# A two-layer mixer trunk on one core: pooling steps dealt out among tiles, two plain tiles ahead of the first seven-product pair, value-row transposes in another bank

## The chip, the cores and the metric

The kernel runs on one core of one Trainium2 chip. The metric is the device time of one execution in microseconds. TensorE (PE, with its weight loads PEld), VectorE (DVE), ScalarE (ACT), GpSimd (POOL) and the DMA queues each run their own instruction stream; streams meet at semaphores.

## The reference, cut to what matters

Two layers run over 640 tokens (128 context, 512 latent), model width 1024. Per layer:

```python
h = rmsnorm(x, norm1_g) * (1 + sc1) + sh1
attn, conv, pool, sgu = four mixers of h @ w_in          # widths 512 each
for i in range(4):                                       # gates and branches
    merged += sigmoid(h @ w_gate[i] + b_gate[i]) * (branch[i] @ w_branch[i])
x = x + g1 * (merged @ w_out)
h = rmsnorm(x, norm2_g) * (1 + sc2) + sh2
x = x + g2 * (square(relu(h @ w_mlp_in)) @ w_mlp_out)    # hidden width 4096
```

The pooling mixer takes 4 groups of 128 channels. For each it forms a centred window sum (windows 2, 4, 8, 16), divides by the number of tokens in the window, subtracts the token itself and multiplies by a 128x128 matrix. The convolution mixer is depthwise with 31 taps, then a layer norm over 512 channels. Attention needs the values by rows (tokens on partitions), while the kernel holds everything else with channels on partitions.

## The kernel before, in words

Channels lie on partitions, the 640 tokens on the free axis, in two halves of 320 columns. Every fp32 operand is split into a high and a low part (`split`, L237 to L241: ACT copies the high part `h`, DVE subtracts it to give the low part `l`), and every product takes three matmuls (h·h, h·l, l·h). A full tile (`mtile`) is 8 chunks x 3 x 2 halves = 48 matmuls of 128x320; a branch or output tile has 4 chunks, so 24. It accumulates in tag `ps` of PSUM, of which there are two; `sc`, `pt` and `po` have one each outside attention. A tile can start only when the tile two before it has been evicted from `ps`.

Weights come as slabs of 128x1024 in the order that `_order` writes down, through 4 `raw` buffers and 3 pairs of split buffers, and `advance` loads 3 slabs ahead and splits 2 ahead. The instruction orders of PE and of the SP DMA queue are those of the program text. DVE, ACT and POOL are ordered by a scheduler with priorities (`later(-n)` raises them), except that DVE too has the order of the text from the pooling stage to the middle of the last gates (`byhand`).

**Value rows.** After `qk`, five transposes in `v_rows` (L832) write a tile of tag `sc`, which two ACT copies (L838) and two DVE subtractions (L839) evict. The tile of tag `sc` used just before holds the sum of squares of q (L413) and is read by the reciprocal root's second step (L400). Next on PE is `conv_in(1)`, in half tiles of 24 matmuls, of tag `ps`.

**Pooling and convolution.** The stage is `gates(3)`, four tiles ("p", g), `branch(3)`, `gates(2)` (with `pool_out` in between), `branch(2)`, gates 1, `branch(1)`. The 31 x 4 convolution taps (L982, one DVE instruction each) are dealt out by `tick`: 5 after a gate, 2 after a branch tile, 6 after each of the first two tiles of gates 1, and the rest there. `pool_in` (L1072) evicts a tile with ACT, then writes DVE's additions (L1086, one to four), four small POOL products (L1092), two DVE instructions (L1096) and a split, all in one go, with no tap in between. `branch` evicts each tile with L1134 and adds it with L1136. `conv_out` sums the four convolution results (L992), takes a column sum on PE (L413), subtracts and squares, takes a second column sum, normalises; its three steps are taken after tiles 1, 2 and 4 of gates 1. In layer 0, `tick` also drives `mod_steps`, which puts small matmuls (L446), transposes and DMAs between the tiles.

**The MLP of layer 1 (`fast_mlp`).** Two tiles of hidden channels are made as a pair with seven products of quarter size (12 matmuls each, L651) in place of eight. That takes sums of quarters of the activations (`ta`, `tb`, L625 to L636, made once at the start on DVE and split) and of the weights (`Feed.pair`, L326 to L334, for each pair). Four plain tiles i0 to i3 come first, then 14 pairs, with output tiles (24 matmuls, evicted into `x` by L553) between the products. The first pair has a branch of its own in the text: two products, four output tiles, five products. `Feed` loads and splits all slabs from the first pair on.

```python
take = {(6, 1): 1, (7, 0): 1, (7, 1): 0}     # output slabs that a pair carries, else 2
```

Of the kernel before, what the change touches and what calls it, by code (L numbers as in the profile page):

```python
# [11 lines left out]
AF = mybir.ActivationFunctionType  # L12
# [3 lines left out]
P = 128  # L16
# [6 lines left out]
TH = T // 2  # L23
# [35 lines left out]
def _pairs():  # L59


    due = [(b, mp) for b in range(6) for mp in range(4)]
    take = {(6, 1): 1, (7, 0): 1, (7, 1): 0}
    r = []
    for b in range(1, 8):
        for p in range(2):
            n = take.get((b, p), 2)
            r.append((b, p, due[:n]))
            del due[:n]
    assert not due  # L70
    return r
# [5 lines left out]
def _order(l):  # L77

    r = [("k", 0), ("v", 0)] + [("q", i) for i in range(4)] + [("a", i) for i in range(8)]
    gate = lambda b: [("g", b, m) for m in range(8)]  # L80
    branch = lambda b: [("b", b, m) for m in range(4)]
    r += gate(0) + [("sv", i) for i in range(4)] + branch(0) + [("u", i) for i in range(4)]
    r += gate(3) + [("p", i) for i in range(4)] + branch(3)
    r += gate(2) + branch(2) + gate(1) + branch(1)
    r += 2 * [("o", m) for m in range(8)]
    if l in FAST:
        r += [("i", j) for j in range(4)]
        for b, p, fs in PAIRS:
            r += [("i", 4 * b + 2 * p + i) for i in range(2)] + [("h", *f) for f in fs]
        return r + 2 * [("f", 3, m) for m in range(8)]  # L90
    r += [("i", j) for j in range(8)]
    for b in range(4):
        if b < 3:
            r += [("i", 8 * (b + 1) + j) for j in range(8)]
        r += [("f", b, m) for m in range(8)] * (2 if b == 3 else 1)
    return r
# [17 lines left out]
def _run(g):  # L114

    try:
        while True:
            next(g)
    except StopIteration as e:
        return e.value  # L120
# [19 lines left out]
def trunk(ctx, tc, a, o):  # L140
# [436 lines left out]
    def first(keys, h, ss1, ab, keep=None):  # L577

        g = mtiles(keys, h, BY_CHUNK if ss1 is None else BY_HALF)
        while True:  # L580
            try:
                at = next(g)
            except StopIteration as e:
                return e.value
            if ss1 is not None and at == (0, 2):
                normed(h, 1, norm_stats(ss1), *ab, keep=keep)
            if nxt["cap"] == 2 and at == (1, 1):
                tick()
                tick()
            if nxt["cap"] == 2 and at == (1, 3):  # L590
                flush()
                pool.dma_start(out=lcol[1], in_=a["cols"][1])
                nxt["cap"] = len(order)

    def fast_mlp(l, mp, h, ss1, ab, fslot, relu2):

# [4 lines left out]
        keep = [ys[c % 4][:, TH * (c // 4):TH * (c // 4) + TH] for c in range(KC)]  # L601
        vs = first([("i", j) for j in range(3)], h, ss1, ab, keep)
        fd = Feed(mp)
        fd.base = fd.slab = nxt["use"] + 1
        todo, i = [], fd.base
        for b, p, fs in PAIRS:
            todo.append(fd.pair(i, [i + 2 + n for n in range(len(fs))]))
            i += 2 + len(fs)
        fd.tail = {n: fd.plain(n) for n in range(i, len(order))}
        fd.pump(2)  # L610
        f = [relu2(v) for v in vs]

        v = _run(mtile(use("i", 3), h))
        feed.append(fd)
        fd.pump()
        f.append(relu2(v))


        tslot = maker(mp, "t", 16, T)
# [37 lines left out]
                vec.tensor_tensor(out, v, s, ALU.add)  # L657
            return out

        fs_, due = {0: f}, []  # L660
        for (b, p, outs), q in zip(PAIRS, todo):
            nxt["use"] += 2 + len(outs)
            ks = dict(zip(outs, q["f"]))
            for n, (fb, mp_) in enumerate(outs):
                for m in (2 * mp_, 2 * mp_ + 1):
                    due.append((fb, m, nxt["use"] - len(outs) + n, ks[fb, mp_]))

            def out_tile():
                if not due:
                    return  # L670
                fb, m, n, k = due.pop(0)
                w = tuple(z.rearrange("p (k c) -> p k c", c=P) for z in ready[n])
                v = _run(mtile(w, fs_[fb], k0=4 * (m % 2)))
                for half in range(2):
                    residual(x[m], v[:, HALVES[half][0]:], mod3(l, 5), m, half)
                if m % 2:
                    ready.pop(n)
                    fd.finish(k)

            if (b, p) == PAIRS[0][:2]:  # L680
                p1, r1, c1, c2 = prod("pt", q["w1"], 0, b11), tmp(TH), tmp(T), tmp(T)
                with later(-EVAC_FIRST):
                    act.activation(r1, p1, AF.Copy)
                plus(prod("sc", q["w1"], 4, b21), r1, c1[:, a0:a1])
                fd.finish(q["k1"])
                for _ in range(4):
                    out_tile()
                p3 = prod("sc", q["w2"], 4, b22)
                p5 = prod("po", q["w4"], 0, t1)
                u2 = plus(prod("pt", q["w2"], 0, t2), r1)  # L690
                fd.finish(q["k2"])
                u3 = plus(prod("pt", q["w3"], 0, t3), u2)
                plus(p5, u2, u2)
                plus(p5, u3, c2[:, b0:b1])
                plus(p3, u2, c1[:, b0:b1])
                plus(prod("pt", q["w3"], 4, t4), u3, c2[:, a0:a1])
                fd.finish(q["k3"])
            else:
                p1, r1 = prod("pt", q["w1"], 0, b11), tmp(TH)
                with later(-EVAC_FIRST):  # L700
                    act.activation(r1, p1, AF.Copy)
                p5 = prod("po", q["w4"], 0, t1)
                out_tile()
                u2 = plus(prod("pt", q["w2"], 0, t2), r1)
                c1 = tmp(T)
                plus(prod("sc", q["w1"], 4, b21), r1, c1[:, a0:a1])
                fd.finish(q["k1"])
                out_tile()
                u3 = plus(prod("pt", q["w3"], 0, t3), u2)
                c2 = tmp(T)  # L710
                plus(p5, u2, u2)
                plus(p5, u3, c2[:, b0:b1])
                out_tile()
                plus(prod("pt", q["w3"], 4, t4), u3, c2[:, a0:a1])
                fd.finish(q["k3"])
                plus(prod("sc", q["w2"], 4, b22), u2, c1[:, b0:b1])
                fd.finish(q["k2"])
                out_tile()
            fb = fs_.setdefault(b, [])
            for c in (c2, c1):  # L720
                s = tmp(T)
                vec.scalar_tensor_tensor(s, c, 0.0, c, ALU.max, ALU.mult)
                fb.append(split(s, fslot, T))
            fb[-2:] = fb[:-3:-1]
# [16 lines left out]
    def qk(l, h, ap, pending, between):  # L741
# [88 lines left out]
        pool.dma_start(out=o["nv"][l], in_=vf[:, 0:SEQ])  # L830

        def v_rows():  # L832
            pt = psum("sc")
            for b in range(5):
                pe.transpose(pt[:, b * P:(b + 1) * P], vf[:, b * P:(b + 1) * P], ident)
            pv = pt[:, 0:T].rearrange("p (b v d) -> p b v d", b=5, v=2)
            for kv in range(NKV):
                act.activation(v5[:, 0:5, kv, 0, :], pv[:, :, kv, :], AF.Copy)  # L838
                vec.tensor_tensor(v5[:, 0:5, kv, 1, :], pv[:, :, kv, :], f5[:, 0:5, kv, 0, :], ALU.subtract)  # L839
# [229 lines left out]
        return split(y, bslot[0], T)  # L1069


    def pool_in(g, h, mk):  # L1072
        v = yield from mtile(use("p", g), h)
        b = tmp(PB)
        for p0, p1 in ((0, PP), (PP + SEQ, 2 * PP + SEQ), (PB - PP, PB)):
# [1 line left out]
        parts = ((0, SEQ, PP), (SEQ, T, 2 * PP + SEQ))  # L1077
        for c0, c1, b0 in parts:
            act.activation(b[:, b0:b0 + c1 - c0], v[:, c0:c1], AF.Copy)
        w = WINDOWS[g]  # L1080
        cur, n, st = b, PB, 1
        bufs = [tmp(PB), tmp(PB)]
        while st < w:
            n -= st
            nx = bufs[0]
            vec.tensor_tensor(nx[:, 0:n], cur[:, 0:n], cur[:, st:st + n], ALU.add)  # L1086
            cur, st = nx, 2 * st
            bufs.reverse()
        off = PP - w // 2
        fx = pfix[:, g * 32:(g + 1) * 32]  # L1090
        for f0, b0 in ((0, 0), (8, SEQ - 8), (16, SEQ + PP), (24, SEQ + PP + LAT - 8)):
# [2 lines left out]
        for c0, c1, b0 in parts:  # L1094
            o0 = b0 - PP + off
            vec.scalar_tensor_tensor(z[:, c0:c1], cur[:, o0:o0 + c1 - c0], 1.0 / w, b[:, b0:b0 + c1 - c0], ALU.mult, ALU.subtract)  # L1096
        return split(z, mk, T)

    def pool_out(l, zs, pw, out):
        for g in range(NG):  # L1100
# [98 lines left out]
    for l in range(DEPTH):  # L1199
# [3 lines left out]
        with opened(f"mx{l}") as mx:  # L1203
# [29 lines left out]
            with opened(f"mg{l}") as mgp:  # L1233
# [14 lines left out]
                with opened(f"pl{l}") as gp:  # L1248
                    mk, wmk = maker(gp, "z", 8, T), maker(gp, "pw", 2, 512)
                    wr = tmp(512)  # L1250
                    pool.dma_start(out=wr, in_=a["pool_w"][l])
                    gs = gates(3, h)
                    pw = split(wr, wmk, 512)
                    zs = [_run(pool_in(g, h, mk)) for g in range(NG)]
                    _run(branch(3, gs, sg, merged, mg))
                    po = []
                    gs = gates(2, h, pool_out(l, zs, pw, po))
                    _run(branch(2, gs, po, merged, mg))
                with opened(f"co{l}") as gp:
# [3 lines left out]
                    for m in range(KC):  # L1263
                        _run(gate(1, m, h, gs))
                        tick(LATE_TAPS if m < 2 else 0)
                        if m == 1:
                            for _ in taps[0]:
                                pass
                            byhand.close()
                        if m in (1, 2, 4):  # L1270
                            next(steps, None)
                    flush()
                    _run(branch(1, gs, co, merged, mg))
# [198 lines left out]
```

## Time and profile before

| | |
|---|---|
| median of 3 runs | 2352.59 us (2351.24 to 2355.08) |
| the profiled execution | 2357.18 us, span 2355.4 us |
| PE busy | 2260.8 us, 96% |
| DVE busy | 1665.2 us, 71% |
| mean granted TensorE clock | 0.989 |

The profiled execution lasted 1.8 us longer than the span of its instructions and 4.6 us longer than the median. PE's busy time is a sum over pipelined matmuls, so a full slice of it is not proof of full speed; the number of matmuls in a stretch and the granted clock say more.

### The profile page before, as it was taken

The page shows a single profiled execution, that of the slowest core. Times are in us where ns is not written, and L with a number is a line of the kernel's source. Part 1 is how long each engine was busy: PE and PEld are TensorE (multiplying, and loading weights), DVE is VectorE, ACT ScalarE, POOL GpSimd, SP SyncE. Part 2 cuts the span into 40 slices and gives each one's busy share as a digit, 9 for nine tenths or more (in the row PEclk, how much of TensorE's full clock was granted, in tenths as well). Part 3 has the DMA queues.
Part 4 walks back from the last instruction along what each step waited for, and adds up shares of the span by engine and source line. Part 5 has one row for each costly group of instructions (what it writes and reads, how often), then busy time and mean ns, then how long its engine had stood idle before and what let it go on. Part 6 is the DMA issues. An engine that isn't in the chain of part 4 may idle for free. (4 is left out here: it accounts for less than half of the span.)

```text
span 2355.4 us, 36300 instructions
## 1 busy us (share of the span) xinstructions
PE 2260.8 (96%) x15038; PEld 2187.8 (93%) x15038; DVE 1665.2 (71%) x2572; ACT 858.6 (36%) x1299; POOL 70.5 (3%) x188
## 2 busy tenths in 40 slices
PE   6999999999999999999998999999999989999997
PEld 5899899989999999999998998999999988999997
DVE  6676457689767776666477773687896788777776
ACT  5445442221435322222254553422224452223233
POOL 1100000000000000000011000000000000000001
PEclk9899999999999999999999999999999999999999
DMA  7331122343343444444344112221222431222223
GB/s 281 109 85 55 62 72 99 121 143 126 135 142 118 153 152 152 150 147 143 114 167 113 61 54 71 73 72 63 69 75 86 147 112 68 80 73 81 90 84 114
DMA packets 77687, 254.01 MB, mean 108 GB/s; under 512 B 11857, under 2 KB 12881, under 8 KB 77393
## 3 DMA queue, kind: packets, MB, share of 16 engines
q1 hardware_dynamic: 67024, 226.14, 29.4%
q0 software_dynamic: 9920, 24.89, 3.9%
q8 instruction: 118, 1.93, 0.3%
q10 hardware_dynamic: 576, 0.66, 0.1%
q14 instruction: 49, 0.39, 0.1%
HBM read 240.22 MB, written 10.75 MB: 107 GB/s over the span
## 5 line engine op out<-in xcount | busy, mean ns | idle before, releaser
L361 PE MATMUL ps<-h,h 128*128 128x320 f32 x5232 | 1112.0, 312 | 23.1 <-DVE gx L1134 9.1
L361 PEld LDWEIGHTS ps<-h,h 128*128 128x128 f32 x5232 | 856.5, 189 | 41.4 <-ACT h L239 13.5
L361 PE MATMUL ps<-h,l 128*128 128x320 f32 x3376 | 831.5, 310 | 0.0
L239 ACT ACTIVATE h<-raw 128x1024 fp32r<-128x1024 f32 x340 | 359.9, 1060 | 1000.0 <-PE ps L361 616.6
L240 DVE TENSOR_TENSOR l<-raw,h 128x1024 fp32r<-128x1024 f32 x340 | 415.3, 1222 | 237.4 <-ACT h L239 237.1
L361 PEld LDWEIGHTS ps<-h,l 128*128 128x128 f32 x3376 | 582.9, 189 | 0.0
L361 PE MATMUL ps<-l,h 128*128 128x320 f32 x1520 | 385.4, 309 | 1.6 <-DVE l L240 1.6
L361 PEld LDWEIGHTS ps<-l,h 128*128 128x128 f32 x1520 | 264.7, 188 | 2.2 <-DVE l L240 1.9
L982 DVE SCALAR_TENSOR_TENSOR cv<-cv,cw,cv 128x655 f32<-128x655 f32 x240 | 215.9, 899 | 6.1
L553 DVE SCALAR_TENSOR_TENSOR x<-ps,mod,x 128x128 f32<-128x128 f32 (+2 forms) x260 | 99.9, 435 | 120.4 <-PE ps L361 120.4
L361 PE MATMUL ph<-h,h 128*128 128x320 f32 x768 | 179.8, 318 | 0.1
L361 PEld LDWEIGHTS ph<-h,h 128*128 128x128 f32 x768 | 129.1, 189 | 7.4 <-DVE cv L972 0.3
L361 PE MATMUL ph<-h,l 128*128 128x320 f32 x384 | 118.5, 309 | 0.0
L239 ACT ACTIVATE h<-tmp 128x640 fp32r<-128x640 f32 (+1 forms) x92 | 67.5, 736 | 134.0 <-DVE tmp L1296 69.8
L361 PE MATMUL ps<-bo,h 128*128 128x320 f32 x512 | 96.4, 309 | 1.8 <-DVE mg L1134 1.8
L240 DVE TENSOR_TENSOR l<-pt,h 128x512 fp32r<-128x512 f32 x84 | 57.8, 688 | 41.5 <-ACT h L239 41.2
L651 PE MATMUL pt<-h,h 128*128 128x320 f32 x280 | 77.8, 312 | 7.8 <-DVE tmp L657 7.8
L361 PEld LDWEIGHTS ps<-bo,h 128*128 128x128 f32 x512 | 80.2, 188 | 5.1 <-issue 2.5
L240 DVE TENSOR_TENSOR l<-tmp,h 128x640 fp32r<-128x640 f32 x92 | 74.8, 817 | 12.6 <-ACT h L239 12.6
L239 ACT ACTIVATE h<-pt 128x512 fp32r<-128x512 f32 x84 | 50.2, 598 | 77.1 <-PE pt L866 70.9
L361 PEld LDWEIGHTS ph<-h,l 128*128 128x128 f32 x384 | 72.1, 188 | 0.0
L651 PE MATMUL pt<-h,l 128*128 128x320 f32 x224 | 69.6, 311 | 0.0
(301 smaller groups left out, 2601.9 us busy)
## 6 DMA issues: line engine op xcount, KB each, us to landing
raw<-in_slabs SPq DMA_DIRECT2D x327, 512.0 KB, 3.6
raw<-in_w_modt SPq DMA_DIRECT2D x48, 512.0 KB, 3.6
md<-in_w_mod SPq DMA_DIRECT2D x32, 512.0 KB, 4.4
q<-qd POOLq DMA_DIRECT2D x18, 256.0 KB, 3.2
st<-in_w_mod SPq DMA_DIRECT2D x8, 512.0 KB, 9.9
raw<-in_w_mod SPq DMA_DIRECT2D x8, 512.0 KB, 6.4
x<-in_x SPq DMA_DIRECT2D x8, 320.0 KB, 6.5
qd<-h POOLq DMA_DIRECT2D x8, 320.0 KB, 10.2
```

Source lines behind the costliest of these rows:

```text
L239: act.activation(h, src, AF.Copy)
L240: (eng or vec).tensor_tensor(lo, src, _f(h), ALU.subtract)
L361: pe.matmul(v[:, c0:c1] if half is None else v, w_[:, kk, :], x_[:, c0:c1], start=first and pi == 0, stop=last and pi == 2)
L553: vec.scalar_tensor_tensor(xc[:, c0:c1], v[:, c0 - b0:c1 - b0], gv[:, c, s:s + 1], xc[:, c0:c1], ALU.mult, ALU.add)
L651: pe.matmul(v, w_[:, k0 + k, :], x_, start=k == 0 and pi == 0, stop=k == 3 and pi == 2)
L982: vec.scalar_tensor_tensor(y, b[:, j:j + CO], cw[:, c * CONV_K + j:c * CONV_K + j + 1], y, ALU.mult, ALU.add)
```

## The change

Three edits and what follows from them.

- `v_rows` takes its tile from `ps`.
- Pooling: `pool_in` ends with the ACT copies and hands the rest to a generator, `pool_steps`, which yields after each addition, after the subtraction and after the split (3 to 6 steps a group). `in_turn` puts these steps ahead of the taps, and `tick(4)` is called after each of the four tiles; what is left is dealt out in `branch(3)`. `conv_out`'s second step is taken after tile 3 of gates 1, not 2.
- `fast_mlp`: the pair of hidden tiles 4 and 5 becomes two plain tiles. The order is i0 to i4, output tiles 0 and 1, i5, output tiles 2 and 3, then 13 pairs, all by the general text. The slabs up to ("h", 0, 1) go through `advance`, and `Feed` begins behind them.

```diff
@@ _pairs
+    del due[:2]
     for b in range(1, 8):
-        for p in range(2):
+        for p in range(1 if b == 1 else 0, 2):
@@ _order
-        r += [("i", j) for j in range(4)]
+        r += [("i", j) for j in range(5)] + [("h", 0, 0), ("i", 5), ("h", 0, 1)]
@@ first
-                nxt["cap"] = len(order)
+                nxt["cap"] = NS + ORDER[1].index(("h", 0, 1))
@@ fast_mlp
-        fd.base = fd.slab = nxt["use"] + 1
+        fd.base = fd.slab = nxt["cap"] + 1
...
-        fd.pump(2)
         f = [relu2(v) for v in vs]
-
-        v = _run(mtile(use("i", 3), h))
-        feed.append(fd)
-        fd.pump()
-        f.append(relu2(v))
+        f.append(relu2(_run(mtile(use("i", 3), h))))
+        f1 = [relu2(_run(mtile(use("i", 4), h)))]
+
+        def plain_tile(w, m, fb):
+            v = _run(mtile(w, fb, k0=4 * (m % 2)))
+            for half in range(2):
+                residual(x[m], v[:, HALVES[half][0]:], mod3(l, 5), m, half)
...
-        fs_, due = {0: f}, []
+        w = use("h", 0, 0)
+        for m in range(2):
+            plain_tile(w, m, f)
+        f1.append(relu2(_run(mtile(use("i", 5), h))))
+        fd.pump(2)
+        w = use("h", 0, 1)
+        for m in range(2, 4):
+            plain_tile(w, m, f)
+        feed.append(fd)
+        fd.pump()
+
+        fs_, due = {0: f, 1: f1}, []
...
-            if (b, p) == PAIRS[0][:2]:
-                (the first pair's own order: two products, four output tiles, five products)
-            else:
-                (the general order)
+            (the general order, for every pair)
@@ v_rows
-            pt = psum("sc")
+            pt = psum("ps")
@@ pool_in
-    def pool_in(g, h, mk):
+    def pool_in(g, h, mk, zs):
...
             act.activation(b[:, b0:b0 + c1 - c0], v[:, c0:c1], AF.Copy)
+        return pool_steps(g, b, parts, mk, zs)
+
+    def pool_steps(g, b, parts, mk, zs):
         w = WINDOWS[g]
...
             bufs.reverse()
+            yield
...
-        return split(z, mk, T)
+        yield
+        zs[g] = split(z, mk, T)
+        yield
+
+    def in_turn(queue, rest):
+
+        live = True
+        while queue or live:
+            if queue:
+                if next(queue[0], StopIteration) is StopIteration:
+                    queue.pop(0)
+                    continue
+            elif next(rest, StopIteration) is StopIteration:
+                live = False
+                continue
+            yield
@@ trunk
-                    zs = [_run(pool_in(g, h, mk)) for g in range(NG)]
+                    zs, queue = [None] * NG, []
+                    taps[0] = in_turn(queue, taps[0])
+                    for g in range(NG):
+                        queue.append(_run(pool_in(g, h, mk, zs)))
+                        tick(4)
                     _run(branch(3, gs, sg, merged, mg))
...
-                        if m in (1, 2, 4):
+                        if m in (1, 3, 4):
                             next(steps, None)
```

## Rows read from the trace of the kernel before

**Rows 1.** The page: busy time of each engine over the span.
```profile
PE 2260.8 (96%) x15038; PEld 2187.8 (93%) x15038; DVE 1665.2 (71%) x2572; ACT 858.6 (36%) x1299; POOL 70.5 (3%) x188
```
**Rows 2.** PE's waits over the whole span: total us, times, longest us.
```profile
PE ps L361 <- DVE gx L1134: 9.1, 6, 4.2
PE pt L651 <- DVE tmp L657: 7.8, 6, 3.4
...
PE sc L835 <- DVE u L400: 5.3, 2, 2.7
...
PE sc L413 <- DVE c L992: 2.9, 1, 2.9
```
**Rows 3.** Windows, layer 1 MLP: length, busy (count) PE PEld DVE ACT POOL, clock, DMA.
```profile
1927.00:1950.00 23.00, 16.67 (x99) 15.79 (x98) 23.00 (x44) 7.80 (x11) 0.00 (x0) 0.93 0.37 120
1950.00:1968.00 18.00, 12.80 (x74) 11.92 (x73) 16.55 (x31) 6.69 (x9) 0.00 (x0) 0.91 0.17 59
...
1968.00:2239.00 271.00, 271.00 (x1851) 271.00 (x1850) 199.87 (x337) 77.97 (x93) 0.00 (x0) 1.00 0.26 80
```
**Rows 4.** PE's waits from 1911 to 1968, two of four.
```profile
PE ps L361 <- ACT h L239: 2.5, 1, 2.5
PE ps L361 <- DVE x L553: 2.3, 1, 2.3
```
**Rows 5.** The chain that ended last, 1911 to 1992: start us, us, what.
```profile
1916.25 1.15 DVE l L240
...
1931.66 0.60 DVE raw L334
...
1935.61 0.40 DVE tmp L627
...
1942.68 2.20 DVE l L240 x3
...
1970.01 3.52 PE ps L361 x24
1973.53 1.76 PE pt L651 x12
```
**Rows 6.** Timeline of DVE, pooling's last group and branch(3) of layer 1.
```profile
1617.91 3.48 DVE L1086 TENSOR_TENSOR tmp<-tmp 128x663 f32<-128x663 f32 x4
...
1621.87 1.08 DVE L1096 SCALAR_TENSOR_TENSOR tmp<-tmp,tmp 128x128 f32<-128x128 f32 x2 [0.48 <-POOL tmp L1092]
...
1626.72 0.81 DVE L1134 SCALAR_TENSOR_TENSOR gx<-gx,ps 128x640 f32<-128x640 f32 x1
...
1628.31 1.83 DVE L982 SCALAR_TENSOR_TENSOR cv<-cv,cw,cv 128x655 f32<-128x655 f32 x2
...
1634.53 0.81 DVE L1134 SCALAR_TENSOR_TENSOR gx<-gx,ps 128x640 f32<-128x640 f32 x1
```
**Rows 7.** Windows elsewhere, columns as in the group of windows above.
```profile
98.62:112.27 13.65, 10.29 (x32) 8.05 (x32) 8.03 (x11) 4.83 (x6) 0.43 (x1) 0.50 0.50 124
1269.39:1272.80 3.41, 2.92 (x12) 2.92 (x13) 3.34 (x5) 0.44 (x1) 0.00 (x0) 0.50 0.58 155
1616.00:1651.00 35.00, 30.38 (x195) 29.79 (x193) 31.99 (x38) 6.14 (x8) 0.75 (x4) 0.95 0.20 61
1652.00:1690.00 38.00, 35.30 (x235) 34.25 (x234) 28.55 (x33) 9.71 (x12) 0.00 (x0) 1.00 0.21 66
1764.17:1771.15 6.98, 4.12 (x14) 3.14 (x13) 3.55 (x5) 2.44 (x3) 0.00 (x0) 0.76 0.23 75
```
**Rows 8.** PE's waits from 457.5 to 480, branch(3) of layer 0.
```profile
PE ps L361 <- DVE gx L1134: 2.5, 2, 1.5
```
**Rows 9.** Timeline of PE, the value rows' transposes of layer 1.
```profile
1269.88 1.33 PE L835 MATMUL sc<-ident,tmp 128*128 128x128 f32 x5 [2.67 <-DVE u L400]
```
**Rows 10.** Timeline of DVE behind those transposes.
```profile
1275.54 0.48 DVE L839 TENSOR_TENSOR vt<-sc,vt 128x320 fp32r<-128x320 f32 x1
...
1277.56 1.56 DVE L240 TENSOR_TENSOR l<-gx,h 128x640 fp32r<-128x640 f32 x2
```

More of the change, by code (lines that the diff above doesn't have):

```diff
@@ L671, in out_tile @@
                 fb, m, n, k = due.pop(0)
[L672 to L675, printed above, removed]
+                plain_tile(tuple(z.rearrange("p (k c) -> p k c", c=P) for z in ready[n]), m, fs_[fb])
                 if m % 2:
@@ L678, in out_tile @@
                     fd.finish(k)
-            if (b, p) == PAIRS[0][:2]:
[L681 to L697, printed above, removed]
-            else:
[L699 to L718, printed above, removed]
@@ new lines, in fast_mlp @@
+            p1, r1 = prod("pt", q["w1"], 0, b11), tmp(TH)
+            with later(-EVAC_FIRST):
+                act.activation(r1, p1, AF.Copy)
+            p5 = prod("po", q["w4"], 0, t1)
+            out_tile()
+            u2 = plus(prod("pt", q["w2"], 0, t2), r1)
+            c1 = tmp(T)
+            plus(prod("sc", q["w1"], 4, b21), r1, c1[:, a0:a1])
+            fd.finish(q["k1"])
+            out_tile()
+            u3 = plus(prod("pt", q["w3"], 0, t3), u2)
+            c2 = tmp(T)
+            plus(p5, u2, u2)
@@ L719, in fast_mlp @@
+            plus(p5, u3, c2[:, b0:b1])
+            out_tile()
+            plus(prod("pt", q["w3"], 4, t4), u3, c2[:, a0:a1])
+            fd.finish(q["k3"])
+            plus(prod("sc", q["w2"], 4, b22), u2, c1[:, b0:b1])
+            fd.finish(q["k2"])
+            out_tile()
             fb = fs_.setdefault(b, [])
@@ L1253, in trunk @@
                     pw = split(wr, wmk, 512)
-                    zs = [_run(pool_in(g, h, mk)) for g in range(NG)]
+                    zs, queue = [None] * NG, []
[3 more added lines that the diff above has]
+                        tick(4)
                     _run(branch(3, gs, sg, merged, mg))
+                    assert all(zs)
                     po = []
```

## The prediction

> **What bounds the kernel now.** I read the page first, then PE's waits, then windows and timelines of the stages that the diff touches. The page puts PE at 96% of the span and DVE at 71% [rows 1], so PE sets the end, and the change can only win where PE stands still or runs slowly. The waits say where [rows 2]. Four of the longer entries lie in the touched places: the branch evictions L1134 (9.1 us in six waits), the sums of products L657 (7.8 in six), the reciprocal root's step L400 ahead of the value rows (5.3 in two, one for each layer), and the convolution sum L992 (2.9 in one). In all four it is DVE that comes late. Behind each stage PE is again without waits, as in the 271 us of pairs, where 1851 matmuls follow each other at 0.1464 us each [rows 3]; time won in a stage should therefore reach the end. That rate is my measure: lost time is a stretch less its matmuls at 0.1464.
>
> The clock adds to it. PE was granted half speed (1.2 of 2.4 GHz) for 13.65 us around the value rows of layer 0 and for 3.41 us around those of layer 1 [rows 7], there after 2.67 us of standing still [rows 9]; the window around the convolution sum has a mean of 0.76 and the two at the start of the MLP 0.93 and 0.91 [rows 3, 7], which also are stretches of half speed.
>
> **MLP start.** From 1927 to 1968 PE ran 173 matmuls in 41.0 us; at 0.1464 they need 25.3, so 15.7 is lost [rows 3]. DVE meanwhile is busy 23.0 of 23 and 16.6 of 18 us [rows 3]: the sums of activation quarters, the first pair's weights and the evictions all fall due together. The change makes hidden tiles 4 and 5 by two plain tiles: 96 matmuls in place of 84, 12 x 0.1464 = 1.76 us more for PE, which nothing hides. DVE sheds one pair's work: three wide splits (1.15 each), one narrow split (0.60 for 512 columns, the price of a 512-wide sum), four weight sums (0.60), seven additions of products (0.40), two squares and two splits of 640 columns (2.20 for three, so 0.73) [rows 5], 12.2 in all. It gains two wide splits and the squares and splits of two plain tiles, 2.3 + 2.9 = 5.2. Net 7.0 us less.
>
> More important is when work falls due. Before, the activation sums (28 steps of 0.40 and eight splits of 0.73, 17.1 us [rows 5]) are wanted after i3, two products and four output tiles. Now i4 and i5 (48 matmuls, 7.0 us each, as 3.52 for 24 [rows 5]) also lie ahead, and half the sums are wanted only in the second half of the pair. The wait of 2.5 for the split of the activations from i3 [rows 4] goes, since i4 now stands between. The wait of 2.3 for an eviction into `x` [rows 4] needn't: output tiles still need DVE. I leave it, with one stretch of half speed (1.7, half of 3.4), and take 15.7 - 4.0 - 1.76 = 9.9 us gained. Bounds: 13.9 if nothing is left; 7.0 if all that DVE does there still has to come first. SP: the slabs up to the second output slab now go out by `advance`, and `Feed`'s loads stand behind them in the same queue; they wait only for raw buffers, which are freed by splits of plain slabs, earlier than before. Taken as nothing, and part of the lower bound.
>
> **Pooling.** In layer 1 the stretch from 1616 to 1651 holds 195 matmuls, 28.5 us of work in 35.0: 6.4 lost [rows 7]. The timeline shows why: DVE runs the last group's four additions from 1617.91, waits 0.48 for POOL, subtracts, waits for ACT's high part, and only then, at 1626.72, evicts the first branch tile; two tiles later PE stands for its bank [rows 6]. With the steps dealt out, three additions (2.6) and one wide split (1.15) come first, so that eviction can run at 1621.7, 5.0 earlier. The fourth addition, POOL's wait, the subtraction and the split (0.87 + 0.48 + 1.08 + 0.73 = 3.2) then stand in the queue of DVE among the first two branch tiles, in the place of three taps (2.7). From there DVE sets the pace, as now: two branch tiles cost it 7.81 (1626.72 to 1634.53) [rows 6] and PE 7.04. The eviction of tile 6, on which the next gate waits, comes at 1621.7 + 8.3 + 2 x 7.81 = 1645.6 in place of 1626.72 + 3 x 7.81 = 1650.15. Gain 4.6; bounds 0 (DVE's queue is as late as before) and 6.4. Behind every pooling step now queue evictions, and PE waits for those; this is counted. Layer 0 has waits of 2.5 there [rows 8], and the small matmuls of `mod_steps` give PE other work while DVE catches up: gain 2.5, bounds 0 and 2.5. Four more `tick` calls also move those matmuls, their DMAs on SP and four small DVE additions to earlier tiles; their number stays, and I cost the move at nothing, its cover being the slabs loaded three ahead. Two taps are left over for the middle of gates 1: 1.8 us of DVE.
>
> **Convolution sum.** Layer 1 waits 2.9 for L992 [rows 2] and then runs at half speed; a mean of 0.76 over 6.98 us costs 1.7 [rows 7]. One gate later (7.0 us) the sum is ready even with the two taps more. The second column sum then has one gate to wait in, not two. DVE does four subtractions and three additions of 655 columns for it, about 5.4 if each costs as a 640-wide step (0.73 to 0.87 [rows 5, 6]); under 7.0. Gain 4.6, bounds 2.9 and 4.6.
>
> **Value rows.** The transposes no longer wait for L400: 2.67 in layer 1 [rows 9], 5.3 for both [rows 2]. In layer 1 the half speed of 3.41 us, in which PE is busy 2.92, should go: 1.5. In layer 0 the clock has fallen before the transposes; between 0 and 1.7 (one such stretch) comes back, I take 0.8. New is a wait for the bank: the second half tile of `conv_in(1)` needs the value rows evicted, and their last subtraction ended at 1276.0, 4.8 after the transposes (1269.88 + 1.33) [rows 9, 10]; a half tile lasts 3.52 [rows 5], so 1.3 in each layer, 2.6. Gain 5.3 + 1.5 + 0.8 - 2.6 = 5.0. Bounds: 8.5 gained without the new wait, and a loss, for which see the fourth rival.
>
> **Sum.** 9.9 + 4.6 + 2.5 + 4.6 + 5.0 = 26.6. The profiled execution took 2357.2 us, so 2330.6 for one like it; it lies 4.6 above the median of the runs, and against that median the forecast is 2352.6 - 26.6 = 2326.0.
>
> **Rivals.** *First, the waits move but stay.* If DVE is still the bound, the MLP gives 7.0, pooling half (2.3 and 1.2), the convolution sum 2.9, the value rows nothing: 13.4, so 2339.2. For it: DVE's 23.0 of 23 us [rows 3]. Against: the next pair's first products need only half the sums.
>
> *Second, the clock stays low.* The waits shorten, but the stretches of half speed remain: 1.7 (MLP) + 1.5 + 0.8 (value rows) + 1.7 (convolution) + 1.7 (branch tiles; the mean of 0.95 over 35 us [rows 7]) = 7.4 less, 2333.4. Against it: from 1652 to 1690 the granted clock is 1.00 although PE is idle for 2.7 of 38 us [rows 7]. The Trainium skill ("TensorE: Matmul & The Clock Gate", section "A second HAM failure mode: psum-queue depth-cycling") has a kernel in which short idling between groups of matmuls, while PSUM banks are cycled, made the clock swing; by it the value rows in the two cycled banks would keep their half speed. The trace speaks against that rule in the window just named, which cycles the same two banks.
>
> *Third, slower.* The first pair now runs in the general order, and `Feed`'s buffers come round one step earlier for every pair. If that makes each of the 13 pairs wait once as long as the eviction into `x` did (2.3 [rows 4]), 29.9 us come on top: 2355.9, slower than before. It decides from 26.6 / 13 = 2.0 us a pair. Against it: the 271 us of pairs show no lost time at all [rows 3], though the buffers there pass through every phase.
>
> *Fourth, the value rows do not gain.* DVE may take their subtractions only after all of the rotation of q, which ends at 1277.56 + 1.56 = 1279.1 [rows 10]. The transposes would end near 1267.7, the half tile near 1271.2, and the bank come free at 1279.6: 8.4 of waiting in each layer, 16.8 for the 2.6 counted: 2340.2.
>
> **How the numbers follow.** Forecast 0.56, first rival 0.16, second 0.10, fourth 0.07, third 0.06, and 0.05 that it comes out near no change. The sum of all upper bounds is 13.9 + 6.4 + 2.5 + 4.6 + 8.5 = 35.9, 2316.7; the other end is that of the first and fourth rivals with a little over. Range 2316 to 2342; the forecast's own is 2317 to 2333. A measurement of this kernel can tell about 0.2%, 4.7 us, from no change. Faster by more than that are the forecast and rivals one, two and four, 0.88 with roundings; within it 0.06; slower 0.06.
>
> **What would show it.** Right: from i3 on to the first product no wait over 2.5 us, and 12 matmuls more; the eviction of the first branch tile about 5 us after the last pooling tile's end (10.7 now); no wait for L992; transposes straight behind the sum of squares; granted clock 1.00 at the MLP's start and after the convolution sum. Wrong: PE waiting for L636 or its split in the first pair, for L839's bank for over 2 us, or once in each pair; or the lost time standing further back, in gates 1 or at the first scores of attention.

## The result and the profile after

| | median | runs | ratio to before, 95% interval |
|---|---|---|---|
| before | 2351.91 us | 2350.66 to 2355.08 | |
| after | 2323.01 us | 2318.24 to 2326.15 | 0.9873 [0.9854, 0.9893] |
| after, once more beside the experiments | 2319.33 us | 2318.52 to 2321.25 | 0.9863 [0.9850, 0.9876] |

By these medians the change made the kernel 28.9 us faster, 31.9 in the second comparison; 26.6 were forecast. For the experiments below, a gain is what the ratio gives on the median of before in the same comparison (2351.2 to 2352.1 us); the difference of the two medians is up to 1 us off it. Lines are renumbered in the kernel after: L239 is now L240, L361 is L362, L553 is L554, L651 is L653, L657 is L659, L835 is L826, L839 is L830, L982 is L973, L1086 is L1080, L1096 is L1091, L1134 is L1144. In the kernels with the pooling steps alone or with the convolution's step as well, L1122 and L1134 are L1141 and L1153.

First the page of the profile after, against [rows 1]:

```profile
span 2324.4 us, 36290 instructions
...
PE 2254.2 (97%) x15050; PEld 2182.7 (94%) x15050; DVE 1655.0 (71%) x2557; ACT 856.4 (37%) x1296; POOL 70.4 (3%) x188
```

PE still sets the end, with less time in which it stands. Its waits over the whole span, against [rows 2] (engine, line, waited for: us in total, times, longest):

```profile
PE ps L362 <- DVE x L554: 4.0, 7, 0.9
PE ps L362 <- DVE gx L1144: 3.1, 5, 0.9
...
PE pt L653 <- DVE tmp L659: 2.6, 3, 1.1
...
PE sc L362 <- DVE l L241: 1.9, 1, 1.9
```

The branch evictions are down from 9.1 us to 3.1, the sums of products from 7.8 to 2.6. The waits for the reciprocal root's step ahead of the transposes and for the convolution's sum are gone. The last row is new.

Windows of the same execution (columns as in [rows 3]): the start of the MLP; the stretch around the first branch tiles and the one behind the first column sum of the convolution, both as long as their counterparts in [rows 7]; the start of the last projection; the value rows of layer 1.

```profile
1605.30:1640.30 35.00, 33.66 (x227) 32.94 (x226) 33.02 (x41) 6.70 (x8) 0.75 (x4) 1.00 0.24 76
1755.88:1762.86 6.98, 6.98 (x47) 6.64 (x46) 5.80 (x7) 4.63 (x6) 0.00 (x0) 1.00 0.22 75
1880.00:1940.00 60.00, 60.00 (x411) 60.00 (x410) 52.85 (x94) 31.64 (x49) 0.00 (x0) 1.00 0.22 69
2249.89:2258.28 8.39, 6.00 (x30) 5.48 (x28) 4.67 (x6) 2.24 (x3) 0.00 (x0) 0.80 0.37 125
1251.21:1275.14 23.93, 21.72 (x119) 19.11 (x118) 16.14 (x23) 10.38 (x14) 6.27 (x9) 0.86 0.56 129
```

The start of the MLP now runs 411 matmuls in 60.0 us, 0.146 each: nothing is lost, where before 15.7 us were. Around the branch tiles 227 matmuls stand in 35 us, before 195. The forecast's sum has no place for two stretches: 30 matmuls in 8.4 us at the last projection, and a clock of 0.86 at the value rows.

To see where time goes without the executions' scatter elsewhere, the table cuts each profiled execution at the same matmuls. Value rows run from the first matmul of ("v", 0)'s placing (L818 before) to the first scores; mixers from the first of the spatial gate's products over tokens (L391) to the column sum ahead of the MLP (L408); the MLP of layer 1 from there to the last norm's column sum. The last column adds up the stretches in which the trace has a granted clock of 0.50 (1.2 of 2.4 GHz), without those at the start and the end of the kernel. All in us.

| kernel | value rows 0 | value rows 1 | mixers 0 | mixers 1 | MLP 1 | half speed |
|---|---|---|---|---|---|---|
| before | 28.6 | 25.3 | 377.2 | 367.4 | 449.2 | 34.1 |
| after | 24.7 | 23.9 | 375.5 | 357.9 | 438.5 | 17.1 |
| after, once more | 21.8 | 21.1 | 375.5 | 357.8 | 438.4 | 3.4 |
| value rows alone | 21.8 | 21.1 | 377.2 | 367.3 | 449.4 | 17.1 |
| MLP alone | 25.6 | 28.6 | 377.2 | 365.7 | 437.0 | 23.9 |
| pooling alone | 26.7 | 28.6 | 379.0 | 365.1 | 449.8 | 44.4 |
| convolution's step alone | 25.5 | 25.6 | 377.2 | 362.6 | 451.5 | 27.3 |
| pooling and convolution's step | 25.3 | 26.6 | 375.6 | 357.8 | 449.9 | 23.9 |
| order of the first pair alone | 26.7 | 25.3 | 377.2 | 367.4 | 450.0 | 34.1 |
| after, extra buffer shifted | 21.9 | 21.1 | 375.5 | 357.8 | 434.7 | 0 |
| the same, old order of the first pair | 21.8 | 21.1 | 375.5 | 357.8 | 440.0 | 3.4 |
| the same as the row of 434.7, four plain tiles | 21.8 | 21.1 | 375.6 | 357.9 | 437.2 | 0 |

### The profile page after: what moved, and what is told of

Read it like the earlier page. It is cut to its first block, busy times and chain, and to the rows that moved or that the text cites. A ratio compares the mean times of both kernels' runs of the same rounds, so it can differ in the third digit from the quotient of the medians.

```text
span 2324.4 us, 36290 instructions
## 1 busy us (share of the span) xinstructions
PE 2254.2 (97%) x15050; PEld 2182.7 (94%) x15050; DVE 1655.0 (71%) x2557; ACT 856.4 (37%) x1296; POOL 70.4 (3%) x188
## 3 DMA queue, kind: packets, MB, share of 16 engines
q1 hardware_dynamic: 66592, 224.56, 29.9%
## 4 chain that ended last, share of the span: by engine, by line
PE 66%; issue 24%; DVE 6%; ACT 2%; DMA 1%; POOL 0%; SPq 0%; DVEq 0%; ACTq 0%; POOLq 0%
PE ps L362 44%; PE ph L362 5%; PE pt L653 4%; DVE l L241 2%; PE sc L653 2%; PE pt L857 1%; PE sc L846 1%; PE po L865 1%; PE sc L362 1%; ACT h L240 1%; PE po L653 1%; PE sc L1031 1%; DMA st<-in_w_mod 1%; PE pt L447 1%; PE sc L414 1%
## 5 line engine op out<-in xcount | busy, mean ns | idle before, releaser
L362 PE MATMUL ps<-h,h 128*128 128x320 f32 x5296 | 1119.3, 310 | 12.8 <-ACT gx L1132 4.7
L362 PEld LDWEIGHTS ps<-h,h 128*128 128x128 f32 x5296 | 862.7, 188 | 31.9 <-ACT h L240 12.5
L362 PE MATMUL ps<-h,l 128*128 128x320 f32 x3408 | 835.7, 309 | 0.0
L240 ACT ACTIVATE h<-raw 128x1024 fp32r<-128x1024 f32 x337 | 357.2, 1060 | 976.7 <-PE ps L362 658.8
L362 PEld LDWEIGHTS ps<-h,l 128*128 128x128 f32 x3408 | 585.6, 188 | 0.0
L362 PE MATMUL ps<-l,h 128*128 128x320 f32 x1520 | 384.6, 308 | 0.0
L362 PEld LDWEIGHTS ps<-l,h 128*128 128x128 f32 x1520 | 263.9, 188 | 0.3
L973 DVE SCALAR_TENSOR_TENSOR cv<-cv,cw,cv 128x655 f32<-128x655 f32 x240 | 215.9, 899 | 6.1
L554 DVE SCALAR_TENSOR_TENSOR x<-ps,mod,x 128x128 f32<-128x128 f32 (+2 forms) x260 | 99.8, 434 | 117.9 <-PE ps L362 117.8
L362 PE MATMUL ph<-h,h 128*128 128x320 f32 x768 | 179.6, 318 | 0.0
L362 PEld LDWEIGHTS ph<-h,h 128*128 128x128 f32 x768 | 129.1, 188 | 7.2
L240 ACT ACTIVATE h<-tmp 128x640 fp32r<-128x640 f32 (+1 forms) x92 | 67.5, 737 | 138.7 <-DVE tmp L1311 79.9
L362 PE MATMUL ph<-h,l 128*128 128x320 f32 x384 | 118.5, 309 | 0.0
L362 PE MATMUL ps<-bo,h 128*128 128x320 f32 x512 | 96.5, 309 | 1.8 <-DVE mg L1144 1.8
L241 DVE TENSOR_TENSOR l<-pt,h 128x512 fp32r<-128x512 f32 x84 | 57.9, 689 | 41.5 <-ACT h L240 41.3
L362 PEld LDWEIGHTS ps<-bo,h 128*128 128x128 f32 x512 | 80.2, 188 | 5.1 <-DVE mg L1144 2.4
L240 ACT ACTIVATE h<-pt 128x512 fp32r<-128x512 f32 x84 | 50.3, 599 | 77.1 <-PE pt L857 70.8
L490 DVE SCALAR_TENSOR_TENSOR junk<-raw,sw 128x1024 f32<-128x1024 f32 x48 | 58.8, 1224 | 25.4 <-DMA raw<-in_w_modt 25.2
L653 PE MATMUL pt<-h,h 128*128 128x320 f32 x260 | 71.4, 309 | 2.6 <-DVE tmp L659 2.6
L362 PEld LDWEIGHTS ph<-h,l 128*128 128x128 f32 x384 | 72.1, 188 | 0.0
```

What stands on the lines that cost most here:

```text
L240: act.activation(h, src, AF.Copy)
L241: (eng or vec).tensor_tensor(lo, src, _f(h), ALU.subtract)
L362: pe.matmul(v[:, c0:c1] if half is None else v, w_[:, kk, :], x_[:, c0:c1], start=first and pi == 0, stop=last and pi == 2)
L490: vec.scalar_tensor_tensor(out, w, 0.5, s3[s], ALU.mult, ALU.mult, accum_out=dst[:, c, s:s + 1])
L554: vec.scalar_tensor_tensor(xc[:, c0:c1], v[:, c0 - b0:c1 - b0], gv[:, c, s:s + 1], xc[:, c0:c1], ALU.mult, ALU.add)
L653: pe.matmul(v, w_[:, k0 + k, :], x_, start=k == 0 and pi == 0, stop=k == 3 and pi == 2)
```

## The experiments

**The value rows alone.**

```diff
-            pt = psum("sc")
+            pt = psum("ps")
```

> The kernel before, with the value rows' transposes in the banks of the dense tiles and nothing else changed. Forecast: 5.0 us faster (bounds: 8.5, and a loss). The trace of after already shows no wait for the bank, so without that term of 2.6 it is up to 7.6. What the trace of after leaves in doubt is the clock: there a half-speed stretch of 6.8 us stood in each layer. If that comes with the edit, layer 1 gains the wait of 2.7 and loses about as much to the clock, and the whole is 4 to 5 us. Fourth rival: 12 us slower, with the half tile after the transposes waiting for the evicted value rows. Read from the trace: the gaps ahead of the transposes and of the half tile behind them, and the granted clock there.

Measured: 2343.43 us, ratio 0.9967 [0.9957, 0.9977], so 7.8 us faster than before. The timelines of PE and of DVE around the transposes of layer 1 (start us, us; to hold against [rows 9, 10]):

```profile
1255.12 0.71 PE L835 MATMUL ps<-ident,tmp 128*128 128x128 f32 x5
```

```profile
1256.89 0.48 DVE L839 TENSOR_TENSOR vt<-ps,vt 128x320 fp32r<-128x320 f32 x1
1257.29 0.81 DVE L400 SCALAR_TENSOR_TENSOR u<-sc,u 128x640 f32<-128x640 f32 x1
1258.03 0.48 DVE L839 TENSOR_TENSOR vt<-ps,vt 128x320 fp32r<-128x320 f32 x1
```

The transposes carry no wait, and the two subtractions run on either side of L400, the second one done 2.7 us after the transposes (1258.51 less 1255.83). The half tile behind lasts 3.5, so no bank is waited for. The second subtraction lay behind most of the rotation in the kernel before; the rotation could start first there, since the transposes themselves waited for L400. The fourth rival falls; it had this edit 12 us slower, or 9.2 with the prediction's gain from the clock (5.3 + 1.5 + 0.8 - 16.8). The windows of the two layers' value rows show the clock:

```profile
94.10:115.94 21.84, 19.04 (x119) 17.09 (x118) 16.53 (x24) 11.03 (x15) 5.26 (x9) 1.00 0.57 132
1248.65:1269.75 21.10, 18.88 (x120) 17.20 (x118) 16.04 (x23) 10.38 (x14) 6.16 (x9) 1.00 0.56 134
```

**The MLP edits alone** (`_pairs`, `_order` and `fast_mlp` as in the change, the rest as before).

> The kernel before, with two plain tiles ahead of the first seven-product pair, the first pair in the order of the others, and nothing else changed. Forecast: 9.9 us faster (13.9 if nothing is left of the waits, 7.0 if all that DVE does there has still to come first). The traces' comparison: 13.9 at the start, less some 4 at the last projection's first three tiles, where after waits for the third slab's split (3 us, then half speed), so again about 10, and a wait ahead of the tail's third tile that names the split. First rival: 7.0, third rival: 3 slower, with a wait in each pair.

Measured: 2339.88 us, ratio 0.9952 [0.9939, 0.9964], 11.3 us faster. The table has 437.0 for the MLP against 449.2. PE's waits at the last projection of this kernel:

```profile
PE sc L362 <- DVE l L241: 1.9, 1, 1.9
...
PE sc L362 <- ACT h L240: 0.5, 1, 0.5
```

So the new wait comes with these edits, and the third rival's price is not paid in the pairs: in the kernel after, the windows from 1880 to 1940 (above) and from 1940 to 2190 (1708 matmuls in 250.0 us) hold no lost time.

The edits also remove work that the forecast did not see. In the kernel before, `advance` loads three slabs past i3 and splits two of them, and `Feed` then loads and splits the same slabs again; with `cap` set and `Feed` begun behind it, nothing is fetched twice. The pages of before and of this kernel count it (slab loads, then wide splits on ACT):

```profile
raw<-in_slabs SPq DMA_DIRECT2D x327, 512.0 KB, 3.6
raw<-in_slabs SPq DMA_DIRECT2D x324, 512.0 KB, 3.7
```

```profile
L239 ACT ACTIVATE h<-raw 128x1024 fp32r<-128x1024 f32 x340 | 359.9, 1060 | 1000.0 <-PE ps L361 616.6
L240 ACT ACTIVATE h<-raw 128x1024 fp32r<-128x1024 f32 x337 | 357.0, 1060 | 991.2 <-PE ps L362 618.0
```

The two layers take 2 x 162 = 324 slabs by `_order`, so three of the 327 loads are in vain. Of the three wide splits less, one is the forecast's (three of a pair less two of the plain tiles) and two are those made in vain. They stand where DVE has least time: by the order of the loads and splits, the split at 1916.25 in [rows 5] is one of them, and the next piece of that chain is a load that goes out when this split has freed its `raw` buffer.

```profile
1917.42 4.48 DMA raw<-in_slabs
```

Over the whole MLP, in the stretches of the table, DVE is busy 9.9 us less in this kernel than in before (335.03 against 344.88), where 7.0 were forecast; two splits of 1.22 are 2.4 of it:

```profile
1871.25:2320.41 449.16, 433.39 (x2910) 429.33 (x2909) 344.88 (x593) 159.13 (x212) 0.00 (x0) 0.99 0.29 90
1866.14:2303.09 436.95, 430.79 (x2923) 428.21 (x2921) 335.03 (x578) 156.24 (x209) 0.00 (x0) 1.00 0.29 89
```

No run takes these loads and splits out by themselves. How much of the 11.3 us is theirs, and how much is that of the plain tiles, stays open.

**The pooling steps alone** (`pool_steps`, `in_turn` and `tick(4)`; the convolution's steps stay at 1, 2 and 4).

> The kernel before, with pooling's steps dealt out among the tiles and the convolution's steps left at tiles 1, 2 and 4. Forecast: 4.6 + 2.5 = 7.1 us faster (bounds 0 and 8.9). First rival, DVE as late as before: 3.5. Interaction: two taps more are left for the middle of gates 1, so the convolution sum can be later than before and the wait of 2.9 grow; then it is less than 7.1, and the difference stands at the tile ahead of the column sum.

Measured: 2353.23 us, ratio 1.0002 [0.9992, 1.0013]: no gain that can be told. PE's waits over the whole span:

```profile
PE sc L413 <- DVE c L992: 6.6, 2, 4.7
```

The wait for the convolution's sum was 2.9 in one [rows 2]. It is now 4.7 in layer 1 and 1.9 in layer 0, where there was none: 1.8 and 1.9 more, about the price of the two taps (1.8) that the deal leaves over for gates 1. Half speed goes with it: 6.8 us of it stand at the wait of layer 1, where the execution of before has 3.4, and 3.4 at that of layer 0, where before has none. In the table, mixers 1 gain 2.3 and mixers 0 lose 1.8.

**The convolution's step alone.**

```diff
-                        if m in (1, 2, 4):
+                        if m in (1, 3, 4):
```

> The kernel before, with the convolution's steps at tiles 1, 3 and 4 in place of 1, 2 and 4, and nothing else changed. Forecast: 4.6 us faster (bounds 2.9 and 4.6), with no wait of PE for the convolution's sum of layer 1 and the granted clock at 1.00 behind it. Rival: the second column sum now has one gate to wait in and not two, so the wait moves there: 0 to 2 us faster.

Measured: 2348.89 us, ratio 0.9992 [0.9983, 1.0001]. The stage gives what was forecast, 367.4 less 362.6 = 4.7, and the wait for L992 is gone, without a new one. The time of the whole shows less (1.9, and its interval holds no change); in the profiled execution the MLP, which the edit does not touch, is 2.3 longer than in the one of before, with 17 us of half speed at its start. The branch waits stay, as PE's waits from 1610 to 1660 show:

```profile
PE ps L361 <- DVE gx L1134: 4.7, 2, 4.2
```

**Both together.**

> The kernel before, with pooling's steps dealt out and the convolution's steps at 1, 3 and 4: both edits together. By themselves they gave nothing and about 2 to 3 us (their traces: 0.4 less and 4.8 less in the stages that they touch). Theory now: the deal pushes two taps into gates 1, which makes the convolution's sum late in both layers (4.7 and 1.9 us of waiting); the later step takes exactly this up, so the two together give 9 to 11 us less than before, far over the sum of 2 to 3. Rival: their effects simply add, 2 to 3 us less.

Measured: 2340.40 us, ratio 0.9955 [0.9942, 0.9967], 10.6 us faster, against 1.4 for the sum of the two alone (0.5 slower and 1.9 faster). The MLP, which neither edit touches, was 2.3 longer in the profiled execution of the second, so times of the whole blur this sum. The stages that the edits touch are the better measure: in the table the pair gains 9.6 in layer 1 and 1.6 in layer 0, together 11.2, and the two alone gain 0.5 and 4.7, together 5.2. So some 6 us come from the two standing together. PE's waits from 1580 to 1770, in which both the 4.2 of the branch and the 2.9 or 4.7 of the column sum have gone:

```profile
PE ps L361 <- ACT gx L1141: 2.7, 4, 0.7
PE ps L361 <- DVE gx L1153: 1.3, 3, 0.6
```

**The order of the first pair alone** (four plain tiles as before, the first pair by the general text).

> The kernel before, with the first pair's seven products and four output tiles in the order of the other pairs, and no plain tiles. Theory of the forecast: what gains at the start of the MLP is the time that the two plain tiles give DVE; the order alone wants the sums of activation quarters one product after the start, where DVE has 17.1 us of them to do, so it gains nothing or loses up to 5 us. Rival: the order itself is what gains (half of the sums are wanted later), and this kernel is 5 to 10 us faster than before, and faster than with the plain tiles by their 1.8 us.

Measured: 2352.79 us, ratio 1.0007 [0.9998, 1.0016]: nothing. PE's waits from 1900 to 1960:

```profile
PE po L651 <- ACT h L239: 9.8, 1, 9.8
PE po L651 <- DVE l L240: 3.7, 1, 3.7
```

The product of `t1` is second in this order and stands for the sums that DVE is still making. The waits of the old order appear in one place instead. This kernel still fetches the three slabs twice (327 loads, 340 wide splits), so it tells what the order is worth with that work in the way.

**The extra buffer shifted** (base: the kernel after).

```diff
-            mks = self.w2 if self.n % 4 == 3 else (wh_, wl_)
+            mks = self.w2 if self.n % 4 == 2 else (wh_, wl_)
```

> The kernel after, with the items of the weight queue that take the single extra buffer shifted by one (number 2 of each four in place of 3), and nothing else changed. Theory from the traces: in the kernel after, the third slab of the last projection falls into the extra buffer, which holds the last pair's second combination, the one whose product ends last; before, it got a buffer that was free one product earlier. Then the wait of 3 us at the last projection's third tile and the half-speed stretch behind it go, 3 to 4 us less than after: about 2319. Rival: DVE's queue is the bound there (additions, squares and splits of the last two tiles), the third slab's split is as late, and the time is that of after. Price in the pairs: the phase shifts there too; the third rival of the forecast would see waits in each pair.

Measured: 2315.94 us (2314.40 to 2320.50), ratio 0.9851 [0.9837, 0.9865]; the kernel after in the same comparison took 2319.33. The MLP is 434.7 long, 3.7 less than 438.4. The extra buffer is a fourth pair of split buffers, which `Feed` gives to every fourth item of its queue. The chain is best read on ACT. In the kernel after, two slabs of the last projection are split so (start us, us, and in brackets the idle time and what ended it); by the loads that the two copies wait for, the first is the fourth slab and the second the third, so the two have changed places:

```profile
2248.23 1.06 ACT L240 ACTIVATE h<-raw 128x1024 fp32r<-128x1024 f32 x1 [3.68 <-PE pt L653]
...
2250.36 1.04 ACT L240 ACTIVATE h<-raw 128x1024 fp32r<-128x1024 f32 x1
```

and DVE makes the third slab's low part behind the squares of the last hidden tiles:

```profile
2252.60 1.22 DVE L241 TENSOR_TENSOR l<-raw,h 128x1024 fp32r<-128x1024 f32 x1
```

PE takes the first three tiles in turns, so it wants the third slab's low part at once; that is done at 2253.82 (2252.60 + 1.22), and PE's waits there are the two rows shown with the MLP edits alone. By the source, the third slab goes into the extra buffer, and that held the last pair's second combination, whose product ends last, at about 2249.9; the fourth gets the buffer that the product before has left, and is split first. With the shift it is the second slab that takes the extra buffer, no later than it was split in the kernel after, and the third is split while the last product still runs, in the buffer that the product before has left:

```profile
2241.67 1.06 ACT L240 ACTIVATE h<-raw 128x1024 fp32r<-128x1024 f32 x1 [3.68 <-PE pt L653]
```

PE's waits at this place are then down to 0.4 for a bank, beside one for a product's eviction that all these kernels have:

```profile
PE pt L653 <- DVE tmp L659: 1.0, 1, 1.0
PE sc L362 <- DVE tmp L659: 0.4, 1, 0.4
```

**The kernel after once more.**

> The kernel after once more, unchanged, beside the three others: its time for comparison (about 2323, 29 us less than before), and how far the half-speed stretches at the value rows move from one execution to another: in the profile of after each layer had 6.8 us of half speed there, in that of before with only the value rows changed none. Theory: these stretches belong to the execution and not to the edit, so this profile shows other ones. Rival: the edit in this company always has them.

Measured: 2319.33 us, as above. The value rows take 21.8 and 21.1 us at a granted clock of 1.00, with the same code that had 24.7 and 23.9 in the first profile.

**The old order of the first pair behind plain tiles** (base: extra buffer shifted; the removed branch of `fast_mlp` put back for the first pair).

> The kernel after with the extra buffer's items shifted (its base, 434.7 us from the MLP's column sum to the last one), and the first pair's products and output tiles back in the order that they had before, behind the two plain tiles. Theory: the plain tiles alone give DVE the time, so the order no longer matters and the stage is 434.7 again, within 1 us; the whole about 2316. Rival: the order is needed as well, since the third to sixth output tiles and the sums then fall together; waits of 2 to 6 us come back at the first pair.

Measured: 2322.04 us, ratio 0.9870 [0.9855, 0.9886]; the MLP takes 440.0, 5.3 more than its base. The theory falls. PE's waits from 1925 to 1960, and the window around them:

```profile
PE pt L653 <- DVE tmp L659: 3.0, 3, 1.8
```

```profile
1940.00:1960.00 20.00, 17.02 (x103) 16.26 (x102) 13.09 (x21) 6.13 (x8) 0.00 (x0) 0.91 0.28 79
```

In the old order four products follow each other in the one bank of `pt` (three of the first pair, one of the next) with no output tile between, and three of them wait for an eviction; part of the window runs at the lower clock. Plain tiles in this order, with no slab fetched twice and without the loss at the last projection, bring the MLP from 449.2 to 440.0; the general order takes another 5.3. That order alone, with four plain tiles and the double fetching, takes nothing: it is worth something only together with the other edits of the MLP.

**Four plain tiles** (base: extra buffer shifted; i4 to i7 plain, 12 pairs).

```diff
-    del due[:2]
+    del due[:4]
...
-        r += [("i", j) for j in range(5)] + [("h", 0, 0), ("i", 5), ("h", 0, 1)]
+        r += [("i", j) for j in range(5)] + [("h", 0, 0), ("i", 5), ("h", 0, 1), ("h", 0, 2), ("h", 0, 3), ("i", 6), ("i", 7)]
...
-            mks = self.w2 if self.n % 4 == 3 else (wh_, wl_)
+            mks = self.w2 if self.n % 4 == 0 else (wh_, wl_)
```

> The same base with four plain tiles in place of two, that is all of the first eight hidden tiles plain and one seven-product pair less; the extra buffer's items shifted so that the last projection's third slab again stands in a buffer that is free early. Theory: the first two plain tiles left no wait that a further pair could take away, so this one costs just its 12 matmuls, 1.76 us: the stage 436.5 us, the whole about 2317.7. Rival: something of the start is still bound by DVE, and the stage is no longer than 434.7. If the buffer of the third slab is not the cause of the wait at the tail, that wait of 3 us is back here.

Measured: 2317.88 us, ratio 0.9849 [0.9832, 0.9865], not to be told from its base; the MLP takes 437.2, 2.4 more than 434.7. That is the 1.76 of twelve matmuls and 0.7 more; PE's waits at the start show only two for evictions into `x` (1.1 together), which the base has not. No wait for a split stands at the last projection, with one pair less and the buffer chosen by the same reasoning.

## Why the prediction was right, and where not

**The total.** The three edits alone give 7.8, 11.3 and 10.6 us, together 29.7; the kernel with all three was, by its ratios, 29.9 and 32.2 faster. They lie in different stages and add up within the scatter, since each of these figures has an interval of 2 to 3 us to either side. The forecast of 26.6 was low by some 3 to 6, and its terms were off in both directions.

**MLP start, 9.9 forecast, 11.3 measured.** The size is near, for errors of opposite sign, so in part by luck. The 4.0 that were left over (a wait for an eviction into `x`, one stretch of half speed) do not occur: the start has no lost time, which was the upper bound of 13.9. And 3.7 that no term held are lost at the other end of the stage. The third rival had the right object, the round of `Feed`'s buffers, and put the price in the wrong place: the pairs show none, but at the last projection three slabs are wanted at once. In the table, 449.2 less 434.7 is 14.5 without that loss, a little over that bound. What DVE sheds was priced too low as well, 7.0 against 9.9 measured, because the two splits made in vain were not seen; the first split that [rows 5] shows, at 1916.25, is one of these. That DVE was late there is borne out, but the plain tiles are not shown to be worth the whole term. Reordering and plain tiles were taken as one term, and the experiments bear that out: the order alone gives nothing, and without it 5.3 are missing.

**Pooling 4.6 and 2.5, convolution 4.6: 11.7 forecast, 10.6 measured.** The sum held, the split did not. The timeline of DVE in the kernel after shows the forecast mechanism in layer 1 (against [rows 6]):

```profile
1610.87 0.81 DVE L1144 SCALAR_TENSOR_TENSOR gx<-gx,ps 128x640 f32<-128x640 f32 x1
...
1612.46 0.83 DVE L1080 TENSOR_TENSOR tmp<-tmp 128x649 f32<-128x649 f32 x1
1613.77 1.08 DVE L1091 SCALAR_TENSOR_TENSOR tmp<-tmp,tmp 128x128 f32<-128x128 f32 x2 [0.48 <-POOL tmp L1087]
1614.76 0.81 DVE L1144 SCALAR_TENSOR_TENSOR gx<-gx,ps 128x640 f32<-128x640 f32 x1
```

The stage starts 10.7 us earlier (1493.19 against 1503.89), and the first eviction comes at 1610.87 in place of 1626.72, so 5.15 earlier in its stage, where 5.0 were forecast. But the pooling term is only worth anything because the convolution's step is moved with it: the two taps left over for gates 1, in the forecast a remark of 1.8 us under cover, cost 1.8 and 1.9 of waiting and some half speed when the cover is missing, and eat nearly the whole gain (0.5 left over the two layers in the table). In layer 0, 1.6 came of the 2.5.

**Value rows, 5.0 forecast, 7.8 measured.** The term that failed is the new wait for the bank, 2.6, which was priced from DVE's order in the kernel before (4.8 us from transposes to eviction). The eviction is ordered by when the transposes are ready, and that was what the edit moved; it takes 2.7. Without this term the forecast is 7.6. In layer 1, 25.3 less 21.1 is 4.2, the 2.7 of the wait and the 1.5 of the clock. In layer 0, 28.6 less 21.8 is 6.8, more than the 3.5 forecast (2.7 and 0.8): the execution of before had 13.7 us of half speed there, the most of all, and the six with the transposes in `sc` took 25.3 to 28.6. So the term for the clock depends on the execution, and that 7.6 comes so near to 7.8 is in part luck.

**The clock (second rival).** In the first profile of after the value rows have 6.8 us at a granted clock of 0.50 in each layer (the 0.86 above), as that rival has it. In the five other profiled executions with the transposes in `ps` it is 1.00 there. All six executions with the transposes in `sc` have half speed in both layers, from 3.4 to 13.7 us. The Trainium skill ("TensorE: Matmul & The Clock Gate", section "A second HAM failure mode: psum-queue depth-cycling") would let the swings go on while the two banks are cycled; these five executions speak against it, the first profile does not. What sets the one execution apart stays open.

**First rival.** DVE is busy for 52.85 of 60 us at the MLP's start and no longer without a pause; the waits did not move within the stage. With 11.3 against 7.0 for the MLP and 7.8 against 0 for the value rows it falls.

## What to carry to other kernels

Where one engine's work is dealt out over several stages, price each edit by what is pushed into the next stage, and try the edits singly and together: two edits that gave 5.2 us in their stages when tried alone gave 11.2 as a pair. When items are taken out of a rotating sequence of buffers, count the round through to its last consumer, above all where several are wanted at once. A wait that is priced from the old order of an engine should be worked out again if the edit changes when its input is ready. And count loads and splits against what the program needs, before and after: 327 loads for 324 slabs showed work in vain that no wait names.

## What was not expected of the hardware

Half speed went with the waits. The profile of before has 34.1 us of it between start and end, that of the fastest kernel none; if PE was busy in all of it, half of it is lost, so up to 17 of the 41.5 us between these two spans (2355.4 and 2313.9) came through the clock, an estimate. And the same instructions need not get the same clock: 24.7 us in one execution of the kernel after and 21.8 in the other for the value rows of layer 0.
